# Fewer modulation steps around two stages, and gates and heads' results requested earlier

## The chip, the cores and the metric

The kernel runs on one core of a Trainium2 chip. The metric is the device time of one execution in microseconds (us), as the median of several executions. A core has a matrix engine (TensorE, PE in the profile; its weight loads are the row PEld), three engines for elementwise work (VectorE or DVE, ScalarE or ACT, GpSimd or POOL) and a queue engine (SyncE, SP) that only issues transfers here. Each engine runs its own list of instructions strictly in order: an instruction that waits holds up all that stand behind it on the same engine. Transfers (DMAs) are issued from the lists of SP, ACT and POOL; an issue that waits for its tile to come free holds up the issues behind it in the same way.

## The reference, cut to what matters

One encoder block over 512 tokens of width 2048, in float32. `c` is a single vector, so the modulation is a vector times a 2048 x 12288 matrix.

```python
mod = silu(c) @ w_ada + b_ada              # six vectors: sh1, sc1, g1, sh2, sc2, g2
h = rms_norm(x, norm1_w) * (1 + sc1) + sh1
qa, ka, va, qb, kb, vb, ga, gb = split(h @ w_in)
ya = global_gqa(...)                       # 8 heads
yb = neighbourhood_attention(...)          # 8 heads
merged = sigmoid(ga) * (ya @ w_oa) + sigmoid(gb) * (yb @ w_ob)
x = x + g1 * (merged @ w_out)
h2 = rms_norm(x, norm2_w) * (1 + sc2) + sh2
x = x + g2 * ((silu(h2 @ w_ffn_gate) * (h2 @ w_ffn_up)) @ w_ffn_down)
return rms_norm(x, final_w)
```

## The kernel before, in words

**Products.** Every float32 matrix is split into a high and a low part in TensorE's fast float32 format (`split`, lines 166 to 170: the high part is a copy on ScalarE, line 168, the low part a subtraction on VectorE, line 170). One product is then three matrix instructions (`mm3`, lines 188 to 190): high by high, low by high, high by low. Weights arrive in units of 128 x 1024 numbers (512 KB, the tile `raw`, line 195), four buffers deep, and are split into the tile `whl`, three buffers deep. `form1` runs such units in order and, when the sum in a PSUM bank is complete, calls `evac`. For `w_oa` a `form1` makes two blocks of 128 output features and has two units (half of the inner dimension each); eight `form1` calls, 16 units, make the stage. `group7` does a 2 x 2 block product with seven instead of eight multiplications, which costs VectorE additional sums.

**Stages around the change.** (1) Gates of `gb` and values of the second attention: five `group7` calls, three from `gates7(1)` to `gates7(3)` and two from `values7`. (2) The heads of the second attention in four pairs `hp`: two `form1` calls (queries, keys; 8 units) and two `att_b`. The result of each head is stored to DRAM (`y_d`) from a tile `yo` of the pool `aside`, tag `y`, two buffers. (3) `w_oa`: `ya @ w_oa` times the gates `sg_a`, which were stored in DRAM (12 of 16 before their sigmoid). During this stage the eight results of the second attention come back from `y_d` into a tile `yr` and are split into `yT` (`attended`). (4) `w_ob`: the same with `yT` and `sg_b`; the two gated products are added. (5) `w_out`, with the residual and the second norm.

**The modulation, in steps.** The part of `w_ada` that isn't needed at the start is 128 blocks of 128 x 1024 numbers (512 KB). A *step* (`advance(mods)`, in `ada_acc`, lines 374 to 390) adds one such block times one element of `silu(c)` per row to a sum `acc`, by one VectorE instruction (line 386, or 384 for the first of 16), and requests the next block (`fetch`, line 364, from POOL; from SP in `w_out`). After 16 steps the sum is split, added up over the rows by TensorE and sent to DRAM and back. Steps are spread over the stages: `group7` with `by_steps` does one in all its inner parts but the first, so three each; elsewhere `slot()` does. A slot is called twice per weight unit (in the middle, and at the end in `pump`) and twice per `att_b`:

```python
pace["due"] = min(pace["due"] + pace["rate"], 1.5)
if pace["due"] >= 1 and (fetched or mod["next"] < mod["end"]):
    pace["due"] -= 1
    advance(mods)
```

`mod["end"]` bounds the number of blocks that a stage may request: 15 up to stage 1, 64 up to `w_oa`, 96 up to `w_out`, 128 in the rest. `pump`, at the end of each unit, also runs one entry of the list `later`.

**What sets the order.** The program text isn't the order on the engines. A planner at compile time runs through the program with assumed durations and puts each instruction in its engine's list when it takes it to be ready, earlier text first. `behind` pins an instruction behind the one traced before it on its engine; `reuse_waits="tile"` lets the tiles of a pool wait for just those older tiles whose memory they take.

**Before, in `w_oa`.** `gated` requests a gate in `evac`, so when the product is complete (line 1117, into a tile of the pool `io`, three buffers, which `ada_o` of the modulation uses too). ScalarE then takes its sigmoid (line 1119) and VectorE multiplies (line 1120). `attended` requests a head's result (line 1075, tag `y`, two buffers, shared with `yo`) and splits it in the same pump.

Of the kernel before, what the change touches and what calls it, by code (L numbers as in the profile page):

```python
# [112 lines left out]
def encoder_block(ctx: ExitStack, tc, xp, xT, c, ada1_w, ada2_w, b_ada, norm1_w, w_in, q_norm_w, k_norm_w, bias,  # L113
# [38 lines left out]
    def bank(tag):  # L152
        return ps.tile([P, 512], F32, tag=tag, name=tag, bufs={"mm": 4, "S": 2, "T": 1, "Y": 1}[tag])
# [60 lines left out]

    def slot():
        pace["due"] = min(pace["due"] + pace["rate"], 1.5)
        if pace["due"] >= 1 and (fetched or mod["next"] < mod["end"]):
            pace["due"] -= 1
            advance(mods)
# [125 lines left out]
    s2 = const.tile([P, KT], F32, name="s2")  # L345
    t2 = const.tile([P, KT], F32, name="t2")

    mod = {"mw": None, "loads": 1, "sums": [(p_w0, 1)], "few": False, "delays": (1, 6, 3), "queue": nc.gpsimd, "next": 0, "end": 0}

    def sum_tile():  # L350
        pool, bufs = mod["sums"][0]
# [49 lines left out]
    def row_products(hl, tag, dst, then):  # L401
        y = bank(tag)
        for n, t in enumerate(hl):
            behind(nc.tensor.matmul(y, ones_r, t, start=n == 0, stop=n == 1))

        def keep():
            o = io.tile([P, 512], F32, tag="io", name="ada_o")
            behind(V.tensor_copy(o[0:1, :], y[0:1, :]))
            nc.gpsimd.dma_start(dst, o[0:1, :])
            if then:  # L410
                then()

        soon.append((2 if mod["delays"][2] > 1 else 1, keep))

    def ada_mod(k0, to):

# [267 lines left out]
    def wforms(w, k0, c0, turned=False, late=False):  # L684
        rt = []
        for a in range(2):
            raw, r3 = unit(w, k0 + 2 * a, 2, c0, 512)
            rt.append((raw, r3[:, :, :256], r3[:, :, 256:]))
        (_, b11, b12), (r1, b21, b22) = rt
        ta = wq.tile([P, 1024], F32, tag="ta", name="ta", bufs=ta_bufs[0])  # L690
        tb = wq.tile([P, 1024], F32, tag="tb", name="tb", bufs=1)
        t1, t2_ = (half(ta)[:, a] for a in range(2))
        t3, t4 = (half(tb)[:, a] for a in range(2))
        V.tensor_sub(t1, b12, b11)  # L694
        V.tensor_sub(t2_, b22, t1)  # L695
        V.tensor_sub(t3, b22, b12)
        last_sum[:] = [V.tensor_sub(t4, *((b21, t2_) if turned else (t2_, b21))).ins]
        hl = [wtiles() for _ in range(4)]
        col = lambda e: lambda t: t.rearrange("p (q n) -> p q n", q=2)[:, :, e * 256:(e + 1) * 256]
        blk = lambda e: lambda t: half(t)[:, e]  # L700
        g0 = [t[:, :512].rearrange("p (q n) -> p q n", q=2) for t in hl[0]]
        parts = (b11, (lambda t: t,)), (r1, (col(0), col(1))), (ta, (blk(0), blk(1))), (tb, (blk(0), blk(1)))
        turn = (0, 2, 3, 1) if late else range(4)
        return split7([parts[n] for n in turn], [g0] + hl[1:], [HALVES[n] for n in turn])
# [35 lines left out]
    def group7(wsrc, xs, order, dst, first_group=False, by_tokens=False, by_steps=False):  # L740

        spare_bank = bank("mm") if first_group else None
        bk = {r: bank((FIRST if first_group else BANK)[r]) for r in ORDER}
        for n, s in enumerate(order):
            with tc.high_priority() if first_group and n == 0 else contextlib.nullcontext():
                w = wsrc(s)
            hold.clear()
            if first_group and n == 0:
                forms = latest[:]
                put_off.pop()()  # L750
                hold[:] = forms
            if first_group and n == 1:
                stirred(spare_bank)
            for r in ORDER:
                (wh, wl), (xh, xl) = w[r], xs[s][r]
                for q in range(2):
                    for c in range(2):
                        o = bk[r][:, c * 256:(c + 1) * 256]
                        cs = slice(c * P, (c + 1) * P)
                        first, last = n == 0 and q == 0 and c == 0, n == len(order) - 1 and q == 1  # L760
                        at = (slice(None), q, cs)
                        with after_stir():
                            if by_tokens:
                                mm3(o, xh[at], xl[at], wh[:, q], wl[:, q], first, last, 256, skip_group_check=True)
                            else:
                                mm3(o, wh[at], wl[at], xh[:, q], xl[:, q], first, last, 256, skip_group_check=True)
                if r == ORDER[2] and by_steps and n:
                    advance(mods)
            pump()
        p = {r: b.rearrange("p (c n) -> p c n", c=2) for r, b in bk.items()}  # L770
        (d11, d12), (d21, d22) = dst() if callable(dst) else dst
        with tc.high_priority():
            p1 = io.tile([P, 512], F32, tag="io", name="p1").rearrange("p (c n) -> p c n", c=2)
            S.activation(p1, p[1], AF.Copy)
            if not first_group:
                V.tensor_add(d11, p[2], p1)
            V.tensor_add(d21, p[6], p1)
            V.tensor_add(d12, p[5], d21)
            if not first_group:
                V.tensor_add(d12, p[3], d12)  # L780
            V.tensor_add(d21, p[7], d21)
            V.tensor_add(d22, p[5], d21)  # L782
            V.tensor_sub(d21, d21, p[4])
            if first_group:
                V.tensor_add(d11, p[2], p1)
                V.tensor_add(d12, p[3], d12)
# [173 lines left out]
    def gates7(n):  # L960
        c = []

        def dst():
            c.append(result())
            v = quarters(c[0])
            return (v[:, 0, 0], v[:, 1, 0]), (v[:, 0, 1], v[:, 1, 1])

        group7(lambda s: wforms(w_in, 4 * s, GB + n * 512), hs, range(4), dst, by_steps=True)
        S.activation(c[0], c[0], AF.Sigmoid)
        for f in range(4):  # L970
            nc.scalar.dma_start(sg_b[4 * n + f].rearrange("p (t n) -> p t n", t=2), quarters(c[0])[:, f // 2, :, f % 2])
# [12 lines left out]
    mods.extend(columns_of((8, 12)))  # L984
    for half_gate in gate_of(5, g2_d, "TT"):
        mods.extend((half_gate, iter([None] * 4)))
    mod.update(mw=p_o[0], end=15)
    for n in range(1, 4):
        gates7(n)
    for hh in range(2):  # L990
# [4 lines left out]
    ta_bufs[0] = 2  # L995

    p_w = tc.alloc_tile_pool(name="p_w", bufs=1, side="right")
    mod.update(mw=p_w, sums=[(p_w, 1), (p_w0, 1)], end=64, loads=3)
    fetch()
    p_b = tc.alloc_tile_pool(name="p_b", bufs=1, side="right")  # L1000

# [68 lines left out]

    p_m = []

    def attended(hl, h):
        yr = aside.tile([P, T], F32, tag="y", name="yr")
        nc.sync.dma_start(yr, y_d[h])
        split(*hl, yr)

    later.extend([lambda: None] * 4 + [lambda: pace.update(rate=0.5)])
    for hp in range(4):
        hh, h0 = hp // 2, 2 * hp  # L1080
        qs, ks = [pair(p_b, "q", T + 64, 3) for _ in range(2)], [pair(p_b, "k", T, 3) for _ in range(2)]
# [29 lines left out]
            t, c = divmod(ix[1].start // P, 2)  # L1111
            return self.t[:, t, c * P:(c + 1) * P]

    def gated(src, dst):
        def evac(w, j, b):
            g = io.tile([P, T], F32, tag="io", name="g")
            nc.sync.dma_start(g, src[j])
            if any(src[j] is t for t in sg_a[:12]):
                S.activation(g, g, AF.Sigmoid)
            V.tensor_mul(dst(j), g, b)  # L1120
        return evac

    turn = itertools.cycle(("mm", "mm", "S"))
    later.extend([lambda: None] * 3 + [lambda h=h: attended(yT[h], 8 + h) for h in range(8)])
    pace["rate"] = 0.35
    for j in range(0, KT, 2):
        tag = next(turn)
        form1([w_oa], j * P, 2, ya, [[bank(tag), bank(tag)]], gated(sg_a[j:], lambda e: oa[j // 2][:, e * 512:(e + 1) * 512]))
    while fetched or mod["next"] < mod["end"]:
        advance(mods)  # L1130
    p_w2 = tc.alloc_tile_pool(name="p_w2", bufs=1, side="left", reuse_waits="tile")
    mod.update(mw=p_w2, sums=[(p_w2, 2)], end=96)
    pace["rate"] = 0.5
    mx, mT = [], []
    for j in range(0, KT, 2):
        o = [p_y.tile([P, T], F32, tag="o", name="o", bufs=4) for _ in range(2)]
        tag = next(turn)
        form1([w_ob], j * P, 2, yT, [[bank(tag), bank(tag)]], gated(sg_b[j:], lambda e: o[e]))
        for e in range(2):
            V.tensor_add(o[e], o[e], oa[j // 2][:, e * 512:(e + 1) * 512])  # L1140
        mx.append(pair(p_m, f"m{j // 2}", 1024, 1))
        for e in range(2):
            mT.append(tuple(Tokens(half(t)[:, :, e]) for t in mx[-1]))
            (mh, ml), o3 = (t.t for t in mT[-1]), o[e].rearrange("p (t n) -> p t n", t=2)
            if j + 2 < KT:
                split(mh, ml, o3)
            else:
                V.tensor_copy(mh, o3)
                V.tensor_sub(ml, o3, mh)
# [517 lines left out]
```

## Time and profile before

| | |
|---|---|
| median of 3 executions | 2475.55 us (2474.43 to 2481.24) |
| the profiled execution | 2477.84 us, its span 2476.1 us |
| PE / PEld busy in the span | 2436.0 us (98%) / 2281.0 us (92%) |
| DVE / ACT / POOL busy | 2007.7 us (81%) / 1073.5 us (43%) / 151.7 us (6%) |
| transfers | 461.78 MB, mean 186 GB/s |

The span runs from the first to the last instruction of the profiled execution; 1.74 us of its time lie around it. In a table of windows each engine's busy time in the stretch is followed by the number of its instructions (x) in parentheses; PEclk is the granted clock of TensorE as a share of full speed. In a list of waits a row says which engine's instruction on which line waited for what: us in total, times, longest. In a timeline a row has start, duration, engine, line, operation, out<-in tiles, and in brackets the idle time before it with what ended it. Rows named SPq or ACTq are issues of transfers. A matrix instruction's duration is longer than the distance to the next, since they overlap; the number of them in a window therefore tells more than the busy share.

### The profile page before, as it was taken

What the parts mean: (1) busy time and instruction counts of PE and PEld (TensorE: products, weight loads), DVE (VectorE), ACT (ScalarE), POOL (GpSimd) and SP (SyncE); (2) the same over time, 40 slices, a digit from 0 to 9 for tenths busy, and PEclk for the clock granted to TensorE, in tenths of its full rate; (3) what the DMA queues carried; (4) which work ended last, traced back from release to release, by engine and by line L of the source; (5) the groups of instructions that cost most, each with busy time, mean ns of one, the idle gap of its engine ahead of it and who ended that gap; (6) DMA issues with size and microseconds to landing.
All of it is one profiled execution on the core that took longest, in us unless ns stands there. A gap on an engine that the chain in (4) does not pass through costs nothing.

```text
span 2476.1 us, 42374 instructions
## 1 busy us (share of the span) xinstructions
PE 2436.0 (98%) x17327; PEld 2281.0 (92%) x17327; DVE 2007.7 (81%) x2704; ACT 1073.5 (43%) x1468; POOL 151.7 (6%) x257
## 2 busy tenths in 40 slices
PE   7999999999999999999999999999999999999998
PEld 6888888999888878888999999999999998999997
DVE  8995778989577658757899889898998885687877
ACT  5223455444344533236744444444444454434333
POOL 0100000000011101021000000000000000000010
PEclk9999999999999999999999999999999999999999
DMA  9874222555667777866454454444544456547563
GB/s 361 295 243 154 89 94 84 159 186 182 210 203 241 246 246 244 309 214 212 135 168 153 138 171 146 136 147 143 164 146 155 135 185 213 206 138 246 192 241 130
DMA packets 213731, 461.78 MB, mean 186 GB/s; under 512 B 15152, under 2 KB 59552, under 8 KB 204832
## 3 DMA queue, kind: packets, MB, share of 16 engines
q1 hardware_dynamic: 173872, 308.71, 38.4%
q0 software_dynamic: 30160, 133.77, 15.8%
q10 hardware_dynamic: 9504, 16.58, 1.9%
q8 instruction: 136, 2.23, 0.4%
q14 instruction: 59, 0.48, 0.1%
HBM read 412.84 MB, written 46.17 MB: 185 GB/s over the span
## 4 chain that ended last, share of the span: by engine, by line
PE 70%; DVE 15%; DMA 6%; issue 5%; ACT 2%; POOL 0%; DVEq 0%; ACTq 0%; POOLq 0%; SPq 0%
PE mm L190 14%; PE mm L189 14%; PE mm L188 14%; PE S L190 5%; PE S L188 5%; PE S L189 5%; DVE whl L170 4%; DMA raw<-in_w_down 3%; PE Y L188 3%; PE Y L189 2%; PE Y L190 2%; DVE raw L522 2%; DMA yr<-y 1%; PE T L884 1%; DVE acc L386 1%
## 5 line engine op out<-in xcount | busy, mean ns | idle before, releaser
L168 ACT ACTIVATE whl<-raw 128x1024 fp32r<-128x1024 f32 (+1 forms) x483 | 454.0, 943 | 674.8 <-PE mm L190 293.1
L170 DVE TENSOR_TENSOR whl<-raw,whl 128x1024 fp32r<-128x1024 f32 (+1 forms) x483 | 518.3, 1087 | 155.8 <-ACT whl L168 155.5
L168 ACT ACTIVATE whl<-ta 128x1024 fp32r<-128x1024 f32 x124 | 131.5, 1060 | 183.2 <-PE mm L190 105.9
L168 ACT ACTIVATE whl<-tb 128x1024 fp32r<-128x1024 f32 x124 | 131.4, 1060 | 170.8 <-PE S L190 111.4
L170 DVE TENSOR_TENSOR whl<-ta,whl 128x1024 fp32r<-128x1024 f32 x124 | 151.4, 1221 | 43.6 <-ACT whl L168 43.5
L386 DVE SCALAR_TENSOR_TENSOR acc<-mw,cact,acc 128x1024 f32<-128x1024 f32 x124 | 158.3, 1278 | 4.1 <-DMA mw<-in_ada_w 4.0
L170 DVE TENSOR_TENSOR whl<-tb,whl 128x1024 fp32r<-128x1024 f32 x124 | 151.1, 1218 | 5.4 <-ACT whl L168 5.3
L364 POOL DMA_DIRECT2D mw<-in_ada_w x115 | 61.2, 532 | 1401.4 <-DVE acc L386 995.2
L695 DVE TENSOR_TENSOR ta<-raw,ta 128x512 f32<-128x512 f32 x124 | 85.3, 688 | 62.3 <-DMA raw<-in_w_down 27.8
L694 DVE TENSOR_TENSOR ta<-raw 128x512 f32<-128x512 f32 x124 | 85.3, 689 | 32.5 <-DMA raw<-in_w_down 30.0
L188 PE MATMUL mm<-x56h,whl 128*128 128x256 f32 x336 | 92.8, 276 | 0.2 <-DVE c L782 0.2
L190 PE MATMUL mm<-x56h,whl 128*128 128x256 f32 x336 | 92.5, 275 | 0.0
L189 PE MATMUL mm<-x56l,whl 128*128 128x256 f32 x336 | 92.5, 275 | 0.0
L188 PE MATMUL mm<-x3h,whl 128*128 128x256 f32 x320 | 88.2, 276 | 0.3 <-DVE c L780 0.3
L188 PE MATMUL mm<-whl,s 128*128 128x256 f32 x320 | 88.2, 276 | 0.0
L189 PE MATMUL mm<-x3l,whl 128*128 128x256 f32 x320 | 88.1, 275 | 0.0
L190 PE MATMUL mm<-whl,s 128*128 128x256 f32 x320 | 88.1, 275 | 0.0
L189 PE MATMUL mm<-whl,s 128*128 128x256 f32 x320 | 88.1, 275 | 0.0
L189 PE MATMUL S<-x56l,whl 128*128 128x256 f32 x320 | 88.1, 275 | 0.0
L190 PE MATMUL S<-x56h,whl 128*128 128x256 f32 x320 | 88.1, 275 | 0.0
L190 PE MATMUL mm<-x3h,whl 128*128 128x256 f32 x320 | 88.1, 275 | 0.0
L188 PE MATMUL S<-x56h,whl 128*128 128x256 f32 x320 | 88.1, 275 | 0.0
(1879 smaller groups left out, 8921.1 us busy)
## 6 DMA issues: line engine op xcount, KB each, us to landing
raw<-in_w_in SPq DMA_DIRECT2D x133, 512.0 KB, 4.5
mw<-in_ada_w POOLq DMA_DIRECT2D x115, 512.0 KB, 4.5
raw<-in_w_gate SPq DMA_DIRECT2D x92, 512.0 KB, 4.6
raw<-in_w_up SPq DMA_DIRECT2D x88, 512.0 KB, 4.5
raw<-in_w_down SPq DMA_DIRECT2D x88, 512.0 KB, 5.1
raw<-in_ada_w POOLq DMA_DIRECT2D x29, 1024.0 KB, 7.5
raw<-in_w_out SPq DMA_DIRECT2D x48, 512.0 KB, 5.0
ffd<-c SPq DMA_DIRECT2D x10, 1024.0 KB, 4.8
```

The source lines that it names most:

```text
L168: high = pin(S.activation(hi, src, AF.Copy))
L170: latest[:] = [high, pin(eng.tensor_sub(lo, src, hi))]
L188: nc.tensor.matmul(o, lh, rh, start=start, stop=False, **kw)
L189: nc.tensor.matmul(o, lh, rl, start=False, stop=False, **kw)
L190: nc.tensor.matmul(o, ll, rh, start=False, stop=stop, **kw)
L364: mod["queue"].dma_start(w, ada2_w[n * P:(n + 1) * P, :])
L386: behind(V.scalar_tensor_tensor(acc, part, cact[:, k:k + 1], acc, op0=ALU.mult, op1=ALU.add))
L522: V.scalar_tensor_tensor(raw, raw, 1.0, call, op0=ALU.mult, op1=ALU.mult, accum_out=y)
L694: V.tensor_sub(t1, b12, b11)
L695: V.tensor_sub(t2_, b22, t1)
L884: nc.tensor.transpose(tp[:, k * P:(k + 1) * P], e[:, k * P:(k + 1) * P], ident)
```

## The change

- `slot()` can switch the modulation to its next pool and bound by itself: once all blocks up to `end` are used up, it takes what lies in `mod["then"]`. For the third pool `p_w2` (bound 96) this replaces the loop at the end of `w_oa` that did the remaining steps up to 64, and `p_w2` is opened before `w_oa` instead of after.
- `gates7(1)` does no steps; the first bound falls from 15 to 12, the second from 64 to 48.
- In the heads' stage the rate 0.5 holds from the first slot, where it began with the fifth pump. In `w_oa` it is 0 up to the fourth pump and then 0.5, where it was 0.35.
- `gated` takes its two gate tiles and requests the gates when it is called, which is ahead of the product's weight units in the text. In `w_oa` the tiles are of the pool `p_y`, tag `o`, four buffers; in `w_ob` of the pool `aside`, tags `y` and `go`, two buffers each.
- `attended(h)` requests head `h` and splits head `h - 2`, which was requested two pumps ahead; the tiles alternate between the tags `y` and `go`. The first call is at the fifth pump of `w_oa` (before: the fourth), the last at the fourteenth of sixteen.
- The number of pumps to the last step of a row sum is written differently with the same values.

```diff
     def slot():
         pace["due"] = min(pace["due"] + pace["rate"], 1.5)
+        if mod["then"] and not fetched and mod["next"] == mod["end"]:
+            mod.update(mod["then"].pop())
...
-        group7(lambda s: wforms(w_in, 4 * s, GB + n * 512), hs, range(4), dst, by_steps=True)
+        group7(lambda s: wforms(w_in, 4 * s, GB + n * 512), hs, range(4), dst, by_steps=n > 1)
...
-    mod.update(mw=p_o[0], end=15)
+    mod.update(mw=p_o[0], end=12)
...
-    mod.update(mw=p_w, sums=[(p_w, 1), (p_w0, 1)], end=64, loads=3)
+    mod.update(mw=p_w, sums=[(p_w, 1), (p_w0, 1)], end=48, loads=3)
...
-    def attended(hl, h):
-        yr = aside.tile([P, T], F32, tag="y", name="yr")
-        nc.sync.dma_start(yr, y_d[h])
-        split(*hl, yr)
-
-    later.extend([lambda: None] * 4 + [lambda: pace.update(rate=0.5)])
+    yrs = {}
+
+    def attended(h):
+        if h > 1:
+            split(*yT[h - 2], yrs.pop(h - 2))
+        if h < 8:
+            yrs[h] = aside.tile([P, T], F32, tag=("y", "go")[h % 2], name="yr")
+            nc.sync.dma_start(yrs[h], y_d[8 + h])
+
+    pace["rate"] = 0.5
...
-    def gated(src, dst):
+    def gated(src, dst, tiles):
+        gs = [t() for t in tiles]
+        for g, j in zip(gs, src):
+            nc.sync.dma_start(g, j)
+
         def evac(w, j, b):
-            g = io.tile([P, T], F32, tag="io", name="g")
-            nc.sync.dma_start(g, src[j])
+            g = gs[j]
             if any(src[j] is t for t in sg_a[:12]):
                 S.activation(g, g, AF.Sigmoid)
             V.tensor_mul(dst(j), g, b)
...
+    p_w2 = tc.alloc_tile_pool(name="p_w2", bufs=1, side="left", reuse_waits="tile")
+    mod["then"].append(dict(mw=p_w2, sums=[(p_w2, 2)], end=96))
     turn = itertools.cycle(("mm", "mm", "S"))
-    later.extend([lambda: None] * 3 + [lambda h=h: attended(yT[h], 8 + h) for h in range(8)])
-    pace["rate"] = 0.35
+    gate_tile = lambda: p_y.tile([P, T], F32, tag="o", name="g", bufs=4)
+    later.extend([lambda: None] * 3 + [lambda: pace.update(rate=0.5)] + [functools.partial(attended, h) for h in range(10)])
+    pace.update(rate=0.0)
...
-        form1([w_oa], j * P, 2, ya, [[bank(tag), bank(tag)]], gated(sg_a[j:], lambda e: oa[j // 2][:, e * 512:(e + 1) * 512]))
-    while fetched or mod["next"] < mod["end"]:
-        advance(mods)
-    p_w2 = tc.alloc_tile_pool(name="p_w2", bufs=1, side="left", reuse_waits="tile")
-    mod.update(mw=p_w2, sums=[(p_w2, 2)], end=96)
+        form1([w_oa], j * P, 2, ya, [[bank(tag), bank(tag)]], gated(sg_a[j:], lambda e: oa[j // 2][:, e * 512:(e + 1) * 512], [gate_tile] * 2))
...
-        form1([w_ob], j * P, 2, yT, [[bank(tag), bank(tag)]], gated(sg_b[j:], lambda e: o[e]))
+        form1([w_ob], j * P, 2, yT, [[bank(tag), bank(tag)]], gated(sg_b[j:], lambda e: o[e], [lambda t=t: aside.tile([P, T], F32, tag=t, name="g") for t in ("y", "go")]))
```

More of the change, by code (lines that the diff above doesn't have):

```diff
@@ L346, in encoder_block @@
     t2 = const.tile([P, KT], F32, name="t2")
-    mod = {"mw": None, "loads": 1, "sums": [(p_w0, 1)], "few": False, "delays": (1, 6, 3), "queue": nc.gpsimd, "next": 0, "end": 0}
+    mod = {"mw": None, "loads": 1, "sums": [(p_w0, 1)], "few": False, "then": [], "delays": (1, 6, 3), "queue": nc.gpsimd, "next": 0, "end": 0}
     def sum_tile():
@@ L411, in keep @@
                 then()
-        soon.append((2 if mod["delays"][2] > 1 else 1, keep))
+        soon.append((min(mod["delays"][2], 2), keep))
     def ada_mod(k0, to):
```

## The prediction, made before the change was run

> **What bounds the kernel now.** I read the page first, then the matrix engine's waits, then windows of the stages that the change touches, then the timelines of the engines that these waits name.
>
> ```profile
> span 2476.1 us, 42374 instructions
> ```
>
> ```profile
> PE 2436.0 (98%) x17327; PEld 2281.0 (92%) x17327; DVE 2007.7 (81%) x2704; ACT 1073.5 (43%) x1468; POOL 151.7 (6%) x257
> ```
>
> PE is busy nearly everywhere, so an edit pays only where PE gets its operands late. Windows show where: of two stretches with the same work, the one with fewer matrix instructions lost time.
>
> ```profile
> 440.00:490.00 50.00, 46.85 (x410) 45.92 (x409) 49.48 (x65) 24.51 (x26) 1.59 (x3) 1.00 0.54 160
> 500.00:550.00 50.00, 50.00 (x450) 50.00 (x449) 44.76 (x55) 23.34 (x25) 2.12 (x4) 1.00 0.56 180
> 637.00:687.00 50.00, 50.00 (x254) 43.36 (x253) 28.72 (x45) 21.10 (x39) 3.72 (x7) 1.00 0.60 195
> 868.00:908.00 40.00, 34.87 (x143) 28.14 (x142) 22.93 (x27) 15.17 (x22) 3.67 (x7) 0.91 0.69 216
> 950.00:990.00 40.00, 40.00 (x187) 35.04 (x186) 34.24 (x42) 13.12 (x17) 4.23 (x8) 1.00 0.76 248
> 1100.00:1150.00 50.00, 50.00 (x233) 43.82 (x232) 31.81 (x41) 25.66 (x37) 9.04 (x8) 1.00 0.69 221
> ```
>
> `w_oa` (868 to 908) has 143 where `w_ob` (950 to 990) has 187 in the same 40 us: 44 are missing, at 40/187 = 0.214 us each **9.4 us**. `gates7(1)` (440 to 490) has 410 where the next groups have 450: 40 x 50/450 = **4.4 us**, with VectorE busy 49.48 of 50. No window of the table beside these two lacks matrix instructions. So these 13.8 us are nearly all that the change can win.
>
> **The stall in `w_oa`.** The waits there, first PE's (820 to 910), then those of ACT and DVE (850 to 905), then SP's (835 to 930):
>
> ```profile
> PE mm L188 <- ACT whl L168: 3.5, 1, 3.5
> PE mm L190 <- DVE whl L170: 1.0, 1, 1.0
> PE S L190 <- DVE whl L170: 0.6, 1, 0.6
> ```
>
> ```profile
> ACT g L1119 <- DMA g<-sga: 15.4, 4, 10.3
> ACT y1h L168 <- DMA yr<-y: 10.4, 1, 10.4
> ACT y5h L168 <- DMA yr<-y: 5.9, 1, 5.9
> ```
>
> ```profile
> SPq L1117 <- DMA g1d<-ada_o: 9.8, 2, 6.0
> ...
> SPq L1075 <- DMA y<-yo: 7.6, 1, 7.6
> ```
>
> PE waits for split weights, but the weights aren't late: ACT stands at a gate's sigmoid or at a head's split, 15.4 + 10.4 + 5.9 us in all, and the weight splits queue behind it. Those transfers are late because SP issues them when they are wanted and then has to wait itself: for the store of the last head (`yo`, whose buffer `yr` takes) and for `ada_o` (whose buffer `g` takes). PE rides over the first 10.4 us on split weights in store with 1.0 us lost, and not over the next:
>
> ```profile
> 883.39 0.38 PE L190 MATMUL mm<-ya1h,whl 128*128 128x512 f32 x1
> 887.24 0.80 PE L188 MATMUL mm<-ya2h,whl 128*128 128x512 f32 x1 [3.47 <-ACT whl L168]
> ...
> 892.93 0.61 PE L188 MATMUL mm<-ya3h,whl 128*128 128x512 f32 x1
> 893.36 0.40 PE L189 MATMUL mm<-ya3l,whl 128*128 128x512 f32 x1
> ```
>
> The stall is 3.6 us, and after it the instructions come 0.43 us apart instead of 0.21 until 893.36 (the clock granted in this stage falls to 0.91): about 3.3 us more. With 1.3 at 872 and 1.1 at 902 that is the 9.4.
>
> A rule of the Trainium skill bears on the second half: "TensorE: Matmul & The Clock Gate", section "Part 1: The HAM clock gate (the 'warmup' mystery)", halves the clock after an idle window of about 3.4 us and gives it back after about 3.4 us of work. By it a stall cut below 3.4 us would cost itself alone, and a full one some 1.7 us extra (an estimate from that page), against the 3.3 here; the 1.0 us stall, without slow instructions behind it, agrees.
>
> **Gates and heads' results ahead.** The change removes each late request. A gate takes a tile of its own, asked for before the product's two units, which run for 2 x 24 x 0.214 = 10.3 us; a head's result is asked for two pumps, also 10.3 us, before its split. What they take to land in `w_oa` (median, the last figure):
>
> ```profile
> mw<-in_ada_w POOLq DMA_DIRECT2D x18, 512.0 KB, 5.4
> raw<-in_w_oa SPq DMA_DIRECT2D x12, 512.0 KB, 5.4
> g<-sga SPq DMA_DIRECT2D x14, 256.0 KB, 5.1
> ...
> yr<-y SPq DMA_DIRECT2D x8, 256.0 KB, 5.8
> ```
>
> 5.1 and 5.8 us are within 10.3, so ACT finds them landed in the steady state. Not so at the start: `yr` of head 2 still takes the buffer of the last head's `yo`, and the gates' tiles lie, by the memory plan, where the last heads' softmax tiles were. One wait of up to 7.6 us remains for ACT, and PE rode over 10.4. I keep 1.5 us of the 9.4 as lost; bounds: all won (9.4), nothing won (0) if the wait only moves. Instructions are neither added nor removed: the same 16 gates and 8 results.
>
> **No steps in the first product group.** The three steps on DVE:
>
> ```profile
> 453.34 0.75 DVE L384 TENSOR_SCALAR acc<-mw,cact 128x1024 f32<-128x1024 f32 x1
> ...
> 465.80 1.28 DVE L386 SCALAR_TENSOR_TENSOR acc<-mw,cact,acc 128x1024 f32<-128x1024 f32 x1
> ...
> 473.42 1.28 DVE L386 SCALAR_TENSOR_TENSOR acc<-mw,cact,acc 128x1024 f32<-128x1024 f32 x1
> ```
>
> They take 0.75 + 1.28 + 1.28 = 3.3 us of DVE in a stretch in which it is hardly ever idle, and PE's waits from 440 to 500 are all for DVE:
>
> ```profile
> PE mm L190 <- DVE whl L170: 1.8, 2, 1.1
> PE mm L188 <- DVE c L780: 0.9, 1, 0.9
> PE mm L188 <- DVE c L782: 0.4, 1, 0.4
> ```
>
> The longest (1.1 us, with its restart 1.3) is at 443, ahead of the first step, and stays. Of the other 4.4 - 1.3 = 3.1 us I take **2.4**: the second L170 wait, at 463, has one step of 0.75 us ahead of it, the two L780 and L782 waits have all three. Bounds: 0, if other sums move into the freed time, and 3.1.
>
> **Where the steps go.** From the code: the heads have 80 slots, at rate 0.5 40 chances for 36 steps (13 to 48), used up eight slots before the end, where before 35 came, ending in the last heads. `w_oa` then does 14 to reach 62 (before 64), `w_ob` 16 as before, `w_out` 18 instead of 16. Each step is 1.28 us of DVE and one 512 KB request. The heads' first units have room (28.72 of 50 us busy, 637 to 687), and so has `w_out` (31.81 of 50, 1100 to 1150). The two steps more in `w_out` are issued on SP among its weights, and the last modulation columns arrive some 8 slots later; no window there lost instructions. I put **0.5** for the heads, whose softmax chains use DVE, **0.5** for `w_oa` and **0.3** for `w_out`; bounds: -1 (the last heads are freed of steps) to +4 (three steps fully exposed, 3 x 1.28).
>
> A detail: `due` has climbed to 1.5 when the work runs out, so the first slot of `w_oa` does one step at rate 0. The early units have one step, not none.
>
> **Sum.** -(9.4 - 1.5) - 2.4 + 0.5 + 0.5 + 0.3 = **-9.0 us**. On the profiled execution's 2477.84 us (span 2476.1) that gives 2468.8; the median lies 2.3 us below it, so for the median 2475.55 - 9.0 = **2466.5 us**.
>
> **Rivals.**
>
> *The stall only moves.* ACT still stands once at a tile that lands late, for longer than the weights in store, and pays a stall and slow instructions as at 883: 3.5 + 3.3 = 6.8 stay of the 9.4. For it: the chain from the last head's store through one buffer is kept. Against: the later waits (5.9, and 10.3 for a gate) lose their cause. 2475.55 - 2.6 - 2.4 + 1.3 = 2471.9 us. The Trainium skill's page "DMA: Bandwidth & Descriptors", section "Issuing engines are not separate DMA queues", speaks for this one: all transfers interleave on the same 16 engines, so what is asked earlier takes share from the weights behind it.
>
> *SP stands at the first gates (slower).* In the text the first gates come ahead of the first `w_oa` units on SP, and their tiles come free only with the last heads' softmax. If SP's list has them in that order, no weights arrive under the last heads, and PE loses the products that it now does there:
>
> ```profile
> 822.85 12.53 SPq L195 DMA_DIRECT2D raw<-in_w_oa  x4
> 843.58 1.00 SPq L1117 DMA_DIRECT2D g<-sga  x2
> ```
>
> ```profile
> 827.00:857.00 30.00, 23.20 (x96) 17.22 (x96) 2.04 (x3) 0.00 (x0) 1.00 0.61 196
> ```
>
> (the last row counts PE's instructions into `mm` tiles from 827 to 857). 96 x 0.214 = 20.5 us would be pushed back: 2466.5 + 20.5 = 2487 us; it decides from about half of it on. Against: SP's list follows readiness, not the text:
>
> ```profile
> 443.46 3.02 SPq L1068 DMA_DIRECT2D yr<-y  x2
> ```
>
> are requests whose place in the text is in the fourth pair of heads, 360 us later.
>
> *It does not keep `w_oa`'s start free.* The one leftover step needs a block from the new pool, whose tiles lie under the last queries and keys; if DVE waits in order for it (5.4 us to land, 1.28 to run) in the last softmax, half of these 6.7 us may show: 2466.5 + 3.4 = 2469.9 us.
>
> **How the numbers follow.** Forecast 0.50, stall moves 0.25, SP stands 0.13, leftover step 0.12. A measurement tells 0.3%, 7.4 us, from no change: faster means below 2468.1, slower above 2483.0. The forecast is only 1.6 us inside, so I give it 0.82 for faster; the stall that moves 0.15; the leftover step 0.4; SP none. Faster 0.41 + 0.04 + 0.05 = 0.50. Slower: most of the SP case, 0.12. Same: 0.38. The range goes from 2460 (13.8 won and the last heads freed, 2.0 us) to 2478, which holds the two middle cases and a small part of the slow one; the forecast's own range is 2461 to 2470.
>
> **What would show it.** A window of 40 us in the middle of `w_oa` has about 187 matrix instructions at clock 1.00. ACT's waits for `sga` and for `yr` fall from over 30 us to under 10, and SP no longer waits for `ada_o`. 440 to 490 has some 430 instructions, with DVE below 48 us. Wrong would be: ACT waiting over 10 us in one piece there, the first `w_oa` product later than 830 us, or losses in the heads (over 3 us more than now).

## The result

The changed kernel takes 2467.8 us (median of 17 runs, 2461.96 to 2474.1), the kernel before beside it 2477.3 us (17 runs, 2474.36 to 2484.21). The ratio is 0.9959, with a 95% interval of 0.9951 to 0.9968. The medians are 9.5 us apart (the ratio alone would make it 10.2), where 9.0 were forecast. The profiled execution of the changed kernel, 2474.1 us, is the longest of its 17, so its span tells less than its stages do.

The page of the changed kernel, its span and busy row:

```profile
span 2472.3 us, 42367 instructions
...
PE 2435.4 (99%) x17327; PEld 2280.1 (92%) x17327; DVE 2007.5 (81%) x2704; ACT 1069.9 (43%) x1466; POOL 150.9 (6%) x255
```

PE has the same 17327 instructions. The windows of the changed kernel show where they sit closer; the first is moved by 2.3 us, because this execution reaches `gates7(1)` that much later:

```profile
442.30:492.30 50.00, 48.52 (x432) 48.14 (x432) 47.12 (x62) 25.12 (x27) 0.00 (x0) 1.00 0.48 146
...
637.00:687.00 50.00, 50.00 (x252) 43.30 (x250) 34.79 (x49) 21.09 (x39) 6.26 (x12) 1.00 0.74 250
...
868.00:908.00 40.00, 40.00 (x187) 34.99 (x186) 30.33 (x35) 11.78 (x15) 5.31 (x11) 1.00 0.97 342
```

`w_oa` holds 187 instead of 143, as many as `w_ob`, at clock 1.00: all 44 missing ones are back, 9.4 us. `gates7(1)` holds 432 instead of 410: 22 x 0.111 = 2.4 us. The first 50 us of the heads lost nothing (252 against 254), although VectorE is busy 34.79 us there instead of 28.72.

The waits of the changed kernel, ACT's (850 to 905) and SP's (835 to 930):

```profile
ACT g L1128 <- DMA g<-sga: 12.8, 4, 5.1
...
ACT y6h L168 <- DMA yr<-y: 2.9, 1, 2.9
ACT y4h L168 <- DMA yr<-y: 2.9, 1, 2.9
```

```profile
SPq L1082 <- DMA y<-yo: 5.1, 2, 3.2
```

ACT's longest wait for a gate is 5.1 us (before: 10.3), for a head's result 2.9 (before: 10.4). SP's for the last head's store is 3.2 (before: 7.6), and the one for `ada_o` is gone.

The last product of `w_ob` and the first of `w_out`, on the timelines of PE, first before, then after:

```profile
1012.00 0.38 PE L190 MATMUL mm<-y7h,whl 128*128 128x512 f32 x1
1012.22 0.38 PE L188 MATMUL mm<-whl,m0h 128*128 128x512 f32 x1
```

```profile
1002.23 0.38 PE L190 MATMUL mm<-y7h,whl 128*128 128x512 f32 x1
1002.44 0.38 PE L188 MATMUL mm<-whl,m0h 128*128 128x512 f32 x1
```

The changed kernel is 9.8 us ahead here, and its span ends only 3.8 us earlier. From there on this one execution loses 6.0 us, and late: on ACT's timeline it is still 9.8 us ahead at 2155 us, where the order of instructions has been the same in both kernels for 1000 us. The medians, 9.5 us apart, don't have this loss, so I take it for the spread of single executions; no run shows what makes it.

### The profile page after: what moved, and what is told of

It is laid out like the page before. It is cut to its first block, busy times and chain, and to the rows that moved or that the text cites. A ratio compares the mean times of both kernels' runs of the same rounds, so it can differ in the third digit from the quotient of the medians.

```text
span 2472.3 us, 42367 instructions
## 1 busy us (share of the span) xinstructions
PE 2435.4 (99%) x17327; PEld 2280.1 (92%) x17327; DVE 2007.5 (81%) x2704; ACT 1069.9 (43%) x1466; POOL 150.9 (6%) x255
## 4 chain that ended last, share of the span: by engine, by line
PE 72%; DVE 14%; issue 6%; DMA 4%; ACT 1%; POOL 0%; DVEq 0%; POOLq 0%; ACTq 0%
PE mm L190 15%; PE mm L189 15%; PE mm L188 15%; PE S L188 6%; PE S L189 6%; PE S L190 6%; DVE whl L170 4%; PE Y L188 3%; PE Y L189 2%; PE Y L190 2%; DVE raw L524 2%; DMA raw<-in_w_down 2%; DMA raw<-in_w_up 1%; PE T L886 1%; DVE g_acc L631 1%
```

## The experiments

The time came out as forecast. The question is whether it came from where the forecast had put it: 7.9 us on the requests for gates and heads' results, nothing on the moved steps. The theory on record is therefore "requests"; its rival is "pause": what cures `w_oa` is that no steps run in the last pair of heads' attention and in the first four units.

| run | kernel | median us | ratio to before (95%) | instructions, 868 to 908 | `w_oa`, us | last store, us (share) |
|---|---|---|---|---|---|---|
| before | | 2477.3 | 1 | 143 | 100.8 | 7.6 (0.98) |
| after | the whole change | 2467.8 | 0.9959 (0.9951 to 0.9968) | 187 | 91.5 | 2.5 (0.61) |
| e1_steps_only | after, requests as before | 2468.81 | 0.9958 (0.9946 to 0.9971) | 187 | 92.1 | 4.0 (0.67) |
| e2_requests_only | before, both requests ahead | 2475.27 | 1.0001 (0.9989 to 1.0012) | 169 | 95.3 | 7.0 (0.97) |
| e3_gates_only | before, gates ahead | 2474.42 | 0.9996 (0.9985 to 1.0007) | 178 | 96.3 | 6.7 (0.96) |
| e4_heads_only | before, heads' results ahead | 2476.37 | 0.9996 (0.9985 to 1.0007) | 148 | 99.6 | 7.4 (1.02) |
| e5_pause_only | before, pause of the steps | 2468.94 | 0.9965 (0.9955 to 0.9975) | 187 | 91.1 | 2.1 (0.57) |
| e6_group_only | before, no steps in `gates7(1)` | 2480.4 | 1.0011 (1.0001 to 1.0020) | 153 | 99.1 | 7.9 (1.00) |
| e7_no_loads | before, steps there without requests | 2476.06 | 0.9995 (0.9984 to 1.0005) | 168 | 95.4 | 2.6 (0.45) |
| e8_short_steps | before, steps there on 8 columns | 2478.58 | 1.0000 (0.9989 to 1.0011) | 162 | 96.7 | 7.5 (1.02) |
| e9_pause_loads | e5 and four requests | 2482.4 | 1.0035 (1.0022 to 1.0048) | 136 | 105.4 | 8.5 (0.98) |
| e10_pause_work | e5 and VectorE work | 2470.89 | 0.9985 (0.9975 to 0.9995) | 184 | 92.1 | 3.9 (0.63) |
| e11_pause_both | e5 and both | 2474.71 | 0.9994 (0.9984 to 1.0005) | 176 | 97.5 | 6.3 (0.91) |

The last three columns are of one profiled execution each. `w_oa` is the time from PE's first product of `w_oa` to its first of `w_ob`; the last store is that of the last head's result, from its issue to its landing, with the share of the transfer engines in that time. A profiled execution needn't be a typical one: those of e2_requests_only and e11_pause_both are the third fastest of 12 and of 10, that of e8_short_steps the ninth of 10.

### The parts of the change, each alone

**e1_steps_only** takes the requests ahead out of the changed kernel.

```diff
-    def attended(h):
...
+    def attended(hl, h):
+        yr = aside.tile([P, T], F32, tag="y", name="yr")
+        nc.sync.dma_start(yr, y_d[h])
+        split(*hl, yr)
...
-            g = gs[j]
+            g = io.tile([P, T], F32, tag="io", name="g")
+            nc.sync.dma_start(g, src[j])
```

> The new spread of the modulation steps, with gates and heads' results requested as before. Theory R (requests): the loss in w_oa comes from ScalarE standing at tiles requested too late, so it stays: about 145 to 155 matrix instructions in the worst 40 us of w_oa, ScalarE's waits for gates and heads' results over 25 us; only the 2.4 us of the first product group are won, 0.1% faster (0.9985 to 0.9995). Theory S (steps): the loss comes from the steps that lie in w_oa's first units, so it goes with them: 185 or more instructions, 0.9955 to 0.9965.

Measured: 2468.81 us; its interval of the ratio holds that of the whole change. The windows and ACT's waits (850 to 905) of this kernel:

```profile
440.00:490.00 50.00, 48.52 (x433) 48.14 (x432) 47.12 (x63) 24.71 (x27) 0.00 (x0) 1.00 0.47 142
...
868.00:908.00 40.00, 40.00 (x187) 34.98 (x186) 27.46 (x31) 14.66 (x19) 5.25 (x10) 1.00 0.80 284
```

```profile
ACT g L1121 <- DMA g<-sga: 15.5, 5, 7.0
ACT y4h L168 <- DMA yr<-y: 4.0, 1, 4.0
```

Every request is made as late as before, ACT waits as long for gates in all (15.5 us against 15.4), and no instruction is missing. Without the requests ahead the whole gain is there.

**e2_requests_only** is the counterpart: the kernel before with `attended` and `gated` of the change and no other part of it. **e3_gates_only** has `gated` alone, **e4_heads_only** `attended` alone.

```diff
-    later.extend([lambda: None] * 3 + [lambda h=h: attended(yT[h], 8 + h) for h in range(8)])
+    later.extend([lambda: None] * 3 + [functools.partial(attended, h) for h in range(10)])
...
-    def gated(src, dst):
+    def gated(src, dst, tiles):
+        gs = [t() for t in tiles]
+        for g, j in zip(gs, src):
+            nc.sync.dma_start(g, j)
```

> Gates and heads' results requested ahead, with the steps as before. Theory R: about 187 instructions in 40 us of w_oa, at clock 1.00; the first product group as before (410 in 440 to 490); 8 to 9 us faster than before w_out begins, ratio 0.9963 to 0.9972. Theory S: w_oa still loses 5 to 9 us, ratio 0.998 or more.

> Only the gates are requested ahead, heads' results and steps as before. If the heads' results are the root (their buffer waits for the last head's store, 7.6 us on the SP list, and everything behind it on SP is late), w_oa still loses 3 to 8 us. If the gates are the root (15.4 us of ScalarE's waits, and their buffer waits for ada_o), at most 2 us are lost.

> Only the heads' results are requested ahead, gates and steps as before. If the heads' results are the root, w_oa loses at most 3 us, and ScalarE's waits for gates fall too, since SP no longer stands; if the gates are, 5 to 9 us stay lost.

None of the three differs from before; the intervals exclude a gain of more than 0.15%, 3.7 us. In the profiled execution of e2_requests_only 18 instructions are missing instead of 44, and `w_oa` takes 95.3 us, between before and after. ACT's and SP's waits there say why not all is back (850 to 905, and 835 to 925):

```profile
ACT g L1126 <- DMA g<-sga: 13.5, 5, 8.5
ACT y2h L168 <- DMA yr<-y: 8.0, 1, 8.0
```

```profile
SPq L1080 <- DMA y<-yo: 10.7, 2, 9.6
```

ACT stands 8.0 us for the result of head 2 and 8.5 us for a gate, though both requests stand further ahead in the text. SP did not issue them early. It stood 9.6 us at the last head's store, which was issued at 852.07 and took 7.0 us, so the request for head 2 left at 859.1 or later; the gate's left only at 887.27. Behind the first wait, which ends at 866.07, PE stalls 1.88 and 0.56 us (872 to 874); behind the second, 26 us later, 0.49 us. A request that is earlier in the text isn't earlier on the queue, as long as the queue stands at a slow transfer.

**e5_pause_only** has the pause alone:

```diff
-    mod.update(mw=p_w, sums=[(p_w, 1), (p_w0, 1)], end=64, loads=3)
+    mod.update(mw=p_w, sums=[(p_w, 1), (p_w0, 1)], end=48, loads=3)
...
-    later.extend([lambda: None] * 3 + [lambda h=h: attended(yT[h], 8 + h) for h in range(8)])
-    pace["rate"] = 0.35
+    mod["end"] = 64
+    later.extend([lambda: None] * 3 + [lambda: (pace.update(rate=0.5), attended(yT[0], 8))] + [lambda h=h: attended(yT[h], 8 + h) for h in range(1, 8)])
+    pace["rate"] = 0.0
```

> The kernel before, with only the pause of the steps: none in the last pair of heads' attention and in w_oa's first four units but the leftover one (bound 48 up to w_oa, then 64; rate 0, then 0.5). First product group, gates and heads' results as before. Theory P (the pause is what cures w_oa): w_oa loses under 1.5 us, 440 to 490 has 410 instructions as before, 7 to 8.5 us faster, ratio 0.9965 to 0.9972. Rival (pause and first group only help together, through the planner's order): w_oa still loses over 4 us, ratio over 0.998.

Measured: 2468.94 us, -8.7 us by the ratio (0.0035 x 2477) and 8.0 us between the medians (before beside it 2476.9), and `w_oa` full. The cure of `w_oa` is the pause. The edit also raises the rate after the pause from 0.35 to 0.5, since the steps that are put off have to be made up.

**e6_group_only** has the empty `gates7(1)` alone:

```diff
-        group7(lambda s: wforms(w_in, 4 * s, GB + n * 512), hs, range(4), dst, by_steps=True)
+        group7(lambda s: wforms(w_in, 4 * s, GB + n * 512), hs, range(4), dst, by_steps=n > 1)
...
-    mod.update(mw=p_o[0], end=15)
+    mod.update(mw=p_o[0], end=12)
```

> The kernel before with no steps in the first product group alone (bound 12, so three steps later in all that follows). The first group wins 2.4 us (424 or so instructions in 440 to 490), w_oa loses its 6 to 10 us as before: ratio 0.9985 to 0.9995. If it changes w_oa too, three more steps fall there and it loses more.

Measured: slower by 0.11%. Two windows of this kernel, and its PE's longest wait in the heads with the instructions around it:

```profile
440.00:490.00 50.00, 48.52 (x432) 48.14 (x432) 47.11 (x62) 24.71 (x27) 0.00 (x0) 1.00 0.52 158
...
737.00:787.00 50.00, 45.86 (x221) 38.40 (x220) 30.69 (x46) 18.39 (x39) 6.85 (x12) 0.93 0.65 207
```

```profile
746.92 0.38 PE L189 MATMUL mm<-h13l,whl 128*128 128x512 f32 x1
750.65 0.80 PE L404 MATMUL Y<-acch,ones_r 128*128 128x512 f32 x1 [3.35 <-ACT yo L1043]
751.24 0.63 PE L404 MATMUL Y<-accl,ones_r 128*128 128x512 f32 x1
751.67 0.63 PE L190 MATMUL mm<-h13h,whl 128*128 128x512 f32 x1
```

`gates7(1)` gains the 2.4 us (432 instructions). But, by the code, the three steps that it loses shift all later ones, and with them the point at which a modulation sum is added up over its rows (line 404). It now needs the bank `Y` while a head's result still lies in it: PE stands 3.35 us for ACT's copy, and runs at half speed after. ACT came late to that copy because it had itself stood 5.60 us, until 747.95, at a transfer: the values of the attention (`vr`) that it splits on line 168. This window holds 221 instructions where e5_pause_only, with before's steps there, holds 255. The gain is given back by where the sum happens to fall; in the whole change, where the rate is set anew, this window holds 254 and no such stall appears.

### What in the steps does the harm

A step is a 512 KB request, about 1.3 us of VectorE, and a place in two lists. Two kernels take one of these away in the last attention pair and in the first four units of `w_oa`. In **e7_no_loads** these steps reuse the last block, in **e8_short_steps** they work on 8 of 1024 columns:

```diff
+            if not mod["quiet"]:
+                w = mod["last"] = mod["mw"].tile([P, 1024], F32, tag="mw", name="mw", bufs=mod["loads"])
...
+            else:
+                w = mod["last"]
```

```diff
+                c = slice(0, 8 if mod["quiet"] else 1024)
+                behind(V.scalar_tensor_tensor(acc[:, c], part[:, c], cact[:, k:k + 1], acc[:, c], op0=ALU.mult, op1=ALU.add))
```

> The kernel before, but while the last pair of heads' attention and w_oa's first four units run, a step requests no new block and the later step takes the last loaded one again (so about five blocks of the modulation are wrong); VectorE's steps all stay. If the steps hurt through the transfers (848 to 868 has a DMA share of 0.99 to 1.04, and the last head's store takes 7.6 us), w_oa's loss falls under 2 us. If they hurt through VectorE's time, it stays at 5 to 10.

> The kernel before, but in the same stretch a step works on 8 of 1024 columns (so that part of the modulation's sum is left out), with every request as before. If the steps hurt through VectorE's time (1.28 us each, some five of them), w_oa's loss falls under 3 us; if through the transfers, it stays at 5 to 10.

Neither cures it: 168 and 162 instructions, and no gain on the median. For VectorE that is an answer: with nearly all of its time gone, `w_oa` still takes 96.7 us, 5.6 more than in e5_pause_only. In e7_no_loads the requests were not simply taken out: 6 blocks still come between 840 and 870, four of them in one burst at 846. From 848 to 858 the transfer share is 1.04, and a gate requested at 848.74 holds ACT until 856.88, 7.15 us; the last store comes after the burst and takes 2.6 us. So here the chain is late by the gate and not by the store.

So the test was turned round: to e5_pause_only, where `w_oa` is whole, requests and VectorE's work are added apart and together, at four slots from the last attention on. **e9_pause_loads** adds requests (they take the same three buffers as the steps' own blocks, so the requests of these move too), **e10_pause_work** VectorE operations, **e11_pause_both** the two together.

```diff
     def slot():
+        if quiet["at"] >= 0:
+            quiet["at"] += 1
+            if quiet["at"] in (2, 4, 7, 10):
+                dummy()
...
+    def dummy():
+        w = mod["mw"].tile([P, 1024], F32, tag="mw", name="mwd", bufs=mod["loads"])
+        behind(V.memset(w[:, :8], 0.0))
+        mod["queue"].dma_start(w, ada2_w[0:P, :])
```

That is e9_pause_loads; in e10_pause_work the function is

```diff
+    def dummy():
...
+        for _ in range(2):
+            behind(V.scalar_tensor_tensor(quiet["w"], quiet["w"], cact[:, :1], quiet["w"], op0=ALU.mult, op1=ALU.add))
```

> The kernel of e5_pause_only (no steps in the last pair of heads' attention nor in w_oa's first four units), with four requests of 512 KB put back at the second, fourth, seventh and tenth slot counted from that last attention on: each behind a memset of 8 columns on VectorE, whose rows then nobody reads; nothing of the result changes. If the steps' transfers are what delays the store of the last head and the gates, the 40 us of w_oa (868 to 908) lose matrix instructions again, 20 or more of 187, ScalarE stands more than 8 us in one piece, and most of the 8.7 us is gone: 2474 to 2478. If it is VectorE's time or the way that the two go together, the 40 us hold some 185 instructions and the time is 2468 to 2470.

> The kernel of e5_pause_only with two VectorE operations of 128x512 at each of the same four slots, and no request: about 1.4 us of VectorE's time a slot, as a step takes; nothing of the result changes. If VectorE's time in these slots is what delays the heads' results, w_oa's 40 us lose 20 instructions or more and the time goes back to 2474 to 2478. If the transfers do it, 185 or more instructions and 2468 to 2470.

> Requests and VectorE's operations of the two kernels before together, at the same four slots. If either alone brings the stall back, so does this: 2474 to 2478. If neither alone does and the two together do, it is their sum: 2473 or more here with 2470 or less for each alone. If this too stays at 2468 to 2470, what the pause takes away is something that this doesn't put back: the steps' own order of waits (a step's sums that wait for its rows, ahead of the heads' work on VectorE), and not the amount of work or of transfers.

The windows of `w_oa`, of e5_pause_only, e9_pause_loads, e10_pause_work and e11_pause_both in this order:

```profile
868.00:908.00 40.00, 40.00 (x187) 35.00 (x186) 25.77 (x29) 13.30 (x17) 4.45 (x9) 1.00 0.80 255
```

```profile
868.00:908.00 40.00, 33.51 (x136) 27.09 (x135) 25.06 (x31) 12.99 (x19) 7.20 (x14) 0.91 0.83 294
```

```profile
868.00:908.00 40.00, 39.59 (x184) 34.32 (x183) 28.64 (x32) 14.00 (x18) 5.31 (x10) 1.00 0.84 285
```

```profile
868.00:908.00 40.00, 37.99 (x176) 32.61 (x175) 27.74 (x32) 14.56 (x20) 6.91 (x13) 1.00 0.90 315
```

Four requests bring the stall back: 51 instructions, 14.3 us of `w_oa` (105.4 against 91.1), and 13.5 us on the median (2482.4 against 2468.94, of another chip; before took 2476.05 and 2476.9 beside them). VectorE's operations cost 3 instructions, 1.0 us of `w_oa` and 2.0 us on the median. It is the transfers, the added ones and those of the steps that they move. The kernel with both has the stall too, but earlier and smaller: PE stalls 1.96 us until 860.93 and is slow until 864.28, ahead of the window shown, so the 11 instructions missing in it are only a part. `w_oa` takes 97.5 us, 6.4 more than e5_pause_only; the median is 5.8 longer. In it the first request goes out at 836.2 instead of 841.5. That fits a stall that depends on what else is on its way at that moment, but was not tested by itself.

How the transfers do it is seen in the requests issued from 840 to 870 (count, KB of one, median us from issue to landing), of before, e5_pause_only, e9_pause_loads and e10_pause_work:

```profile
mw<-in_ada_w POOLq DMA_DIRECT2D x9, 512.0 KB, 6.4
...
y<-yo ACTq DMA_DIRECT2D x2, 256.0 KB, 5.5
```

```profile
mw<-in_ada_w POOLq DMA_DIRECT2D x5, 512.0 KB, 5.7
...
g<-sga SPq DMA_DIRECT2D x7, 256.0 KB, 3.9
...
y<-yo ACTq DMA_DIRECT2D x2, 256.0 KB, 3.0
```

```profile
mwd<-in_ada_w POOLq DMA_DIRECT2D x3, 512.0 KB, 6.5
g<-sga SPq DMA_DIRECT2D x4, 256.0 KB, 7.2
...
y<-yo ACTq DMA_DIRECT2D x2, 256.0 KB, 8.3
```

```profile
mw<-in_ada_w POOLq DMA_DIRECT2D x4, 512.0 KB, 5.9
...
y<-yo ACTq DMA_DIRECT2D x2, 256.0 KB, 4.0
```

With 5 or 4 blocks of steps in these 30 us a head's store takes 3.0 or 4.0 us (the median of two stores); with 9 it takes 5.5, and with 3 extra ones beside 6, 8.3. The count alone doesn't set it: e11_pause_both also has 3 beside 6, and 4.8. What goes with it is how full the engines are while the store is under way. In before, the two stretches around the last store:

```profile
848.00:858.00 10.00, 10.00 (x53) 8.44 (x52) 7.72 (x13) 4.80 (x8) 2.63 (x5) 1.00 0.99 331
858.00:868.00 10.00, 10.00 (x48) 8.75 (x47) 3.57 (x4) 0.00 (x0) 1.06 (x2) 1.00 1.04 403
```

Over all 13 kernels the last column of the table falls into two groups. At a share of 0.45 to 0.67 the last store takes 2.1 to 4.0 us, and `w_oa` 91.1 to 92.1 (e7_no_loads apart, where a gate is late); at 0.91 to 1.02 it takes 6.3 to 8.5 us, and `w_oa` 95.3 to 105.4. The store of the head before shows that a high share isn't enough by itself: at 0.87 to 0.97 it took 3.5 to 4.3 us in four of the kernels, and 8.0 in e9_pause_loads.

The timelines of ACT and SP show what hangs on the last of these stores, first in before, then in e5_pause_only, then in e9_pause_loads:

```profile
853.01 0.63 ACT L1119 ACTIVATE g<-g 128x512 f32<-128x512 f32 x1 [2.36 <-DMA g<-sga]
...
854.22 0.33 ACTq L1044 DMA_DIRECT2D y<-yo  x1
...
861.86 0.81 SPq L1075 DMA_DIRECT2D yr<-y  x2
...
868.03 0.63 ACT L168 ACTIVATE y1h<-yr 128x512 fp32r<-128x512 f32 x1 [10.37 <-DMA yr<-y]
```

```profile
848.90 0.33 ACTq L1044 DMA_DIRECT2D y<-yo  x1
...
851.00 0.80 SPq L1075 DMA_DIRECT2D yr<-y  x2
...
855.56 0.63 ACT L168 ACTIVATE y1h<-yr 128x512 fp32r<-128x512 f32 x1 [1.55 <-DMA yr<-y]
```

```profile
854.27 0.33 ACTq L1050 DMA_DIRECT2D y<-yo  x1
...
862.86 1.07 SPq L1086 DMA_DIRECT2D yr<-y  x2
...
866.85 0.63 ACT L168 ACTIVATE y1h<-yr 128x512 fp32r<-128x512 f32 x1 [7.46 <-DMA yr<-y]
```

It is a chain of three transfers, each behind the one before: a gate lands, and ACT can go on to the copy of the last head; its store lands, and SP can request a head's result into that buffer; that lands, and ACT goes on to the weight splits. (With the pause the first link is gone: that copy waits 0.22 us for PE and for no transfer.) From the store's issue to SP's next request it is 7.6 us in before, 2.1 with the pause, and 8.6 with the requests put back. The store itself also starts 5.3 us later in before and 5.4 later in e9_pause_loads than with the pause (854.22 and 854.27 against 848.90), some of it because those two executions are 2 to 3 us later at this point. The Trainium skill, page "DMA: Bandwidth & Descriptors", section "Issuing engines are not separate DMA queues", says that transfers of all issuers interleave on the same engines; these rows agree, POOL's requests lengthening ACT's store.

## Why the prediction was right, and where it was not

**The stalls and their size: right.** The 9.4 us of `w_oa` and the 4.4 us of `gates7(1)`, read off the windows, are where the change won; 9.4 and 2.4 of them came back.

**"Gates and heads' results ahead": the step that failed.** The 7.9 us were booked here. The requests ahead alone bring nothing that can be measured (e2 to e4), and without them the gain is whole (e1). The waiting engines were named rightly, ACT at gates and heads' results and SP at the store of `yo`, but the cause was not. The text took the landing times of 5.1 and 5.8 us as given and moved the requests ahead of them. They are not given: the last head's store, 256 KB too, takes 2.1 us in e5_pause_only and 8.5 in e9_pause_loads, with what the steps' blocks do to the share. Nor is "requested two pumps ahead" given: in e2_requests_only SP stood at that store and issued late what the text asks for early. The estimate that one wait of up to 7.6 us remains was near (8.0 there), but PE didn't ride over it: it stalled 1.88 and 0.56 us, and a second wait of 8.5 us came later.

**"Where the steps go": the price that was missed.** Moving the steps was costed at +0.5 for the heads and +0.5 for `w_oa`, with a gain of 1 us as the bound for freeing the last heads (2.0 us in the range). The pause there and in `w_oa`'s first units is worth 8.0 to 8.7 us (e5_pause_only). The text counted a step as 1.28 us of VectorE "and one 512 KB request", and then priced only the VectorE part. The rows that spoke against this stood in the trace of before: from 848 to 868 the transfers ran at a share of 0.99 to 1.04 (shown above), in just the stretch of the store and of a late gate.

**"No steps in the first product group": right,** 2.4 us forecast, 22 instructions or 2.4 us measured. That the steps might cost up to 4 us elsewhere was too low a bound by itself: alone (e6_group_only) it loses 34 instructions in a single window of the heads, 34 x 0.196 = 6.7 us.

**The rivals.** *The stall only moves* is near what the requests ahead do alone, as far as their one trace shows: PE still stalls 1.88, 0.56 and 0.49 us, and `w_oa` takes 3.8 us more than in the changed kernel; in the whole change the pause has removed the cause. *SP stands at the first gates* did not happen: the first product of `w_oa` starts at 827.13 us (before: 827.58). *The leftover step* cost nothing that shows: no wait of PE from 820 to 910 is longer than 0.2 us in the changed kernel.

**What would show it.** 187 instructions at clock 1.00, 432 in `gates7(1)` with VectorE at 47.12, and no wait for `ada_o` are as written. ACT's waits for `sga` and `yr` falling from over 30 us to under 10 are not: 18.6 us stay in the rows shown, and in e1_steps_only 15.5 for gates alone, without a lost instruction. By these rows the sum of the waits is not what costs; I take it to be the single wait that outlasts the split weights in store.

**The total was right by luck, by a swap:** the term of 7.9 us was booked on a step that gains nothing alone, and the moved steps, booked as a cost, bring about as much. With 9.4 instead of 7.9 in `w_oa`, and nothing instead of 1.3 for the moved steps, the sum would be 11.8 us. The medians are 9.5 apart. No run says where the 2.3 us between are; the 17 executions of the changed kernel spread over 12 us.

**What stays open.** Whether e7_no_loads would be cured with its burst at 846 spread out: no run does that. Why a high share made the last store slow and mostly not the one before. And why e2_requests_only, with 26 of 44 instructions back in its profiled execution, has no better median: one trace of each kernel was taken, and its 12 executions spread from 2471.05 to 2483.49 us.

## What to carry to other kernels

Optional background work that loads data has two prices, its engine time and its share of the transfers; at a change of stage, where a store must land before a load and a load before the next weights, the second can be the larger, so pause it there and do it where no chain of transfers hangs on it. Before asking for late data earlier, look at what else is on its way in that stretch, and at what the queue stands at: a request ahead in the text isn't issued ahead while its queue waits for a slow transfer. And when parts of a change go together, test each alone before crediting one, even when the total comes out as forecast.

## What the runs showed of the hardware

**A full transfer share alone need not stop the matrix engine.** In the changed kernel `w_oa` runs at a transfer share of 0.97 and 342 GB/s (window above) without a lost matrix instruction, more than the 0.69 of before, which lost 44. Here it mattered when the share was high and which chain hung on a transfer then: in before it was 0.99 to 1.04 from 848 to 868, ahead of the loss.

**The matrix clock fell after shorter stalls than 3.5 us too, and not after each.** PE's timeline in e9_pause_loads:

```profile
896.95 0.38 PE L189 MATMUL S<-ya0l,whl 128*128 128x512 f32 x1
899.94 0.48 PE L190 MATMUL S<-ya0h,whl 128*128 128x512 f32 x1 [2.61 <-DVE whl L170]
900.26 0.38 PE L188 MATMUL S<-ya0h,whl 128*128 128x512 f32 x1
900.48 0.38 PE L189 MATMUL S<-ya0l,whl 128*128 128x512 f32 x1
...
901.44 0.63 PE L190 MATMUL S<-ya0h,whl 128*128 128x512 f32 x1
901.87 0.63 PE L188 MATMUL S<-ya0h,whl 128*128 128x512 f32 x1
...
904.43 0.49 PE L188 MATMUL S<-ya1h,whl 128*128 128x512 f32 x1
```

A stall of 2.61 us is enough here. The instructions right after it still come 0.22 us apart, and only from 901.44 to 904.43 are they 0.43 apart: 7 intervals, about 1.5 us more. The stall's length doesn't decide it alone: in e11_pause_both one of 1.96 us (until 860.93) is followed at once by instructions 0.43 us apart until 864.28, and in e9_pause_loads one of 2.93 us (until 851.56) by none. The prediction had drawn from the Trainium skill, page "TensorE: Matmul & The Clock Gate", section "Part 1: The HAM clock gate (the 'warmup' mystery)", that a stall below some 3.4 us costs itself alone. These two traces do not agree, and the measurement decides; the 3.5 us stall of before, with its 3.3 us extra, is the dearest case here.
